# Moving the operands of every large matmul to multiples of 512 bytes

## The chip, the cores and the metric

The kernel runs on one core of a Trainium2 chip. What counts is the device time of one execution in microseconds (us), as the median of several runs. Five engines work side by side from queues of their own: TensorE (PE; its weight loads are shown apart, as PEld), VectorE (DVE), ScalarE (ACT), GpSimd (POOL) and SyncE (SP, which here only issues DMAs). SBUF is the on-chip memory from which all of them read: 128 partitions, each a row of bytes with addresses of its own. In this text the offset of a buffer is the place in that row where it begins.

## The reference

One layer over 256 tokens of width 2048, all in float32: a mixer with three recurrent branches, a cross attention over 256 memory tokens, and a gated feed-forward part. Each is wrapped in an RMS norm and added back.

```python
h = rms_norm(x, norm_mix_pre)
z = h @ w_in                                  # 2048 -> 14368 columns
y_a = gated_delta_rule(...) @ w_dn_out        # chunks of 64 tokens, triangular solves
y_b = gla_chunked(...) @ w_gla_out
y_c = split(gelu(s5_ssm(...)) @ w_s5_glu)
x = x + rms_norm((g_a*y_a + g_b*y_b + g_c*y_c) @ w_mix_out, norm_mix_post)
x = x + rms_norm(cross_attention(rms_norm(x), rms_norm(mem), w_xa_q, w_xa_kv, w_xa_out), norm_xa_post)
gate, up = split(rms_norm(x, norm_ffn_pre) @ w_ffn_up)          # 2048 -> 2 x 5632
x = x + rms_norm((gelu(causal_conv(gate)) * up) @ w_ffn_down, norm_ffn_post)
```

## The kernel before

Nearly all of the arithmetic is matrix products with weights that are read once from HBM. Each float32 factor is split into a high part, rounded to the matmul type float32r, and the rest (`whi`/`wlo` for weights, the two halves of `aa`, `ach`/`acl` and others for activations). A product is then three matmuls: high by high, high by low, low by high.

`load_w` (L198 on) brings two slices of 128 rows by 512 columns into `raw`, and ACT and DVE split them into `whi` and `wlo` (both on L204). Two routines use them:

- `proj` (L226) keeps the weights stationary. `mm3` (L207) issues for each 128x128 block one matmul with `whi`, through which both halves of the activation run as two separate stretches of 256 columns (L216, at the end of a sum L219), and one with `wlo`, through which the high half runs, 256 columns (L217). Such a wide and narrow matmul are called a pair here. There are 64 pairs in a slab of 512 output columns.
- `proj_tok` (L263) keeps the activation stationary and lets 512 columns of `whi`, `whi` and `wlo` run through it, each in one stretch (L283, L284, L285). For a part of `w_kv` it is 256 columns.

The stages follow each other: the columns of `w_in` by `proj` and `proj_tok`, with the recurrent branches in pieces between their matmuls; the branches' output products (with stationary tiles of the pool `s16`, named `f`, and of `aa`); `w_mix` (stationary `mgx`); the cross attention (`aa`, `xq`, `xo_`); 22 slabs of `w_up` by `proj` (moving `aa`); four slabs of `w_down` by `proj_tok` (stationary `ach` and `acl`).

Where a buffer lies is set by the tile pools. A pool of the left side begins where the pool below it ends, one of `side="right"` ends where the one above it begins, and each buffer begins at the next multiple of 32 bytes. The order in which instructions stand on each engine is set when the program is built. In the program as built these are the offsets, as the rest after division by 512:

| buffer | used by | rest before |
|---|---|---|
| `whi`, `wlo` | every product | 96 |
| `aa` | stages up to `w_up` | 96 |
| `f` (`s16`) as stationary | output product of the first branch | 96 |
| `xset`, `xq`, `mgx`, `ach`, `acl` | first stage, attention, `w_mix`, `w_down` | 480 |
| `xo_` | attention output | 64 |

Slices of these buffers begin at further multiples of 512, so all operands taken from one of them share its rest. 96 and 480 are odd multiples of 32; 64 is a multiple of 64.

Of the kernel before, what the change touches and what calls it, by code (L numbers as in the profile page):

```python
# [9 lines left out]
F32 = mybir.dt.float32  # L10
FR = mybir.dt.float32r
# [7 lines left out]
P = 128  # L19
T = 256  # L20
# [3 lines left out]
NW = 512  # L24
# [31 lines left out]
V_CONV = 64  # L56
# [6 lines left out]
V_LIM = V_LRE + 32  # L63
V_LST = V_LIM + 32
V_N = V_LST + 32


def _constants():
# [18 lines left out]
class Net:  # L87
# [21 lines left out]
    def setup(self):  # L109
        self.cp = self.ctx.enter_context(self.pool("cp"))  # L110
        self.ps_acc = self.ctx.enter_context(self.pool("ps_acc", bufs=N_ACC, space=PSUM))
        self.ps_mx = self.ctx.enter_context(self.pool("ps_mx", bufs=8 - N_ACC, space=PSUM))
        self.dram = self.ctx.enter_context(self.pool("dram", space=DRAM))
        self.cst = self.cp.tile([P, C_N], F32, name="cst")
        self.vec = self.cp.tile([P, V_N], F32, name="vec")
        self.ident = self.cst[:, C_ID:C_ID + P]
        self.ones = self.cst[:, C_ONE:C_ONE + P]

# [887 lines left out]
def tile_kernel(ctx, tc, consts, vecs, ab, gla_up, s5_br, s5_bi, s5_cr, s5_ci, post_rows,  # L1006
                x_tok, xT, memT, w_in, w_small, w_dn, w_gla, w_glu, w_mix, w_q, w_kv, w_xo, w_up, w_down, out):
    nc = tc.nc
    n = Net(ctx, tc)
    n.setup()  # L1010
    n.open_weights()
    dram = n.dram
    hpool = ctx.enter_context(n.pool("hp"))

    def set_a(dt=FR):
        return hpool.tile([P, 2, KD, T], dt, name="aa", tag="aa")
# [18 lines left out]
    def xr(k, m=1):  # L1035
        return xh2[k // 8][:, k % 8:k % 8 + m, :] if m > 1 else xh2[k // 8][:, k % 8, :]
# [7 lines left out]
    def x_load(c):  # L1044
        a, b = chs[c]
        nc.sync.dma_start(out=xr(a, b - a), in_=xT[:, a:b, :])

    def hold_dma(ap):
        with n.after(n.prev):
            nc.vector.memset(ap, 0.0)  # L1050

    def x_split():
        for c, (a, b) in enumerate(chs):
            if c < 4:
                x_load(c + 1)
            for k in range(a, b):
                nc.scalar.activation(xs_[:, 0, k, :], xr(k), AF.Copy, scale=n.v_(V_MIXPRE, k))
                n.seq(lambda: nc.vector.scalar_tensor_tensor(xs_[:, 1, k, :], xr(k), n.v_(V_MIXPRE, k),
                                                             xs_[:, 0, k, :].bitcast(F32), op0=ALU.mult,
                                                             op1=ALU.subtract))  # L1060
                made0.append(k)
                yield 0.4
            if c == 3:
                hold_dma(n.cst[:, 0:1])
                nc.sync.dma_start(out=n.cst, in_=consts)
            if c == 4:
                hold_dma(n.vec[:, V_CONV:V_CONV + 1])
                nc.sync.dma_start(out=n.vec[:, V_CONV:], in_=vecs[:, V_CONV:])
            if c:
                a = max(b - 4, 0)  # L1070
                n.norm_acc(n.s4, xr(a, 4).rearrange("p k s -> p (k s)"), xacc, c == 1)
            yield 1.1
# [16 lines left out]
    x_load(0)  # L1089
    nc.sync.dma_start(out=n.vec[:, :V_CONV], in_=vecs[:, :V_CONV])  # L1090
    e0 = n.spawn(x_split(), R_X)
    n.hp = 0
    n.seq_on = True
# [158 lines left out]
    cc = c_stack.enter_context(n.pool("cc"))  # L1252
# [3 lines left out]
    xn = cc.tile([P, 2, D], F32, name="xn")  # L1256
    n.side.dma_start(out=xn, in_=x_tok.rearrange("(t p) e -> p t e", t=2))
    kT = cc.tile([P, 4, T], F32, name="kT")
    n.t2 = c_stack.enter_context(n.pool("ct2", bufs=2))

    def post_row(q, s):
# [58 lines left out]

    nb = n.spawn(norm1(), R_N1)
    n.gate = True
    vt = cc.tile([P, 2, NW], F32, name="vt")

    def v_part(c0, c1):
        n.proj_tok(w_kv[1][:, :, c0:c1], KD, lambda k: (mh[:, k, :], ml[:, k, :]),
                   lambda t, acc: nc.scalar.activation(vt[:, t, c0:c1], acc, AF.Copy, scale=rm_col[:, t:t + 1]),
                   c1 - c0)
# [2 lines left out]
           lambda m, acc: nc.vector.tensor_mul(kT[:, m, :], n.total(acc), rm_row))  # L1331
    if VS:
        v_part(0, VS)
    qT = cc.tile([P, 4, T], F32, name="qT")

    def q_rhs(k):
        n.finish(nb, lambda: k in made)
# [9 lines left out]
    at = cc.tile([P, KD, T], F32, name="at", tag="yg")  # L1347
    pr_ = at[:, 0:8, :].rearrange("p (h t) s -> p h t s", h=4)
    pT = at[:, 8:16, :].rearrange("p (h m) s -> p h m s", h=4)
    xo_ = cc.tile([P, 2, 4, T], FR, name="xo_")  # L1350
    xoh, xol = xo_[:, 0], xo_[:, 1]
    with tc.high_priority(HPA):
        for h in range(4):
# [218 lines left out]
```

## Time and profile before

| | |
|---|---|
| median of three runs | 1955.02 us (1954.22 to 1959.61) |
| the profiled execution's own time | 1953.59 us |
| its span, first to last instruction | 1951.8 us |
| PE busy | 1889.8 us (97%) |
| DVE busy | 1420.0 us (73%) |
| ACT busy | 951.8 us (49%) |
| DMA engines busy, mean | about 60% |
| granted TensorE clock, mean | 0.992 |

The time a matmul is shown to take includes the way through the array and overlaps the next one, so a busy PE tells little of its pace. The pace is read from the starts: the distance from one matmul's start to the next in an unbroken run.

### The profile page before, as it was taken

The page shows a single profiled execution, that of the slowest core. Times are in us where ns is not written, and L with a number is a line of the kernel's source. Part 1 is how long each engine was busy: PE and PEld are TensorE (multiplying, and loading weights), DVE is VectorE, ACT ScalarE, POOL GpSimd, SP SyncE. Part 2 cuts the span into 40 slices and gives each one's busy share as a digit, 9 for nine tenths or more (in the row PEclk, how much of TensorE's full clock was granted, in tenths as well). Part 3 has the DMA queues.
Part 4 walks back from the last instruction along what each step waited for, and adds up shares of the span by engine and source line. Part 5 has one row for each costly group of instructions (what it writes and reads, how often), then busy time and mean ns, then how long its engine had stood idle before and what let it go on. Part 6 is the DMA issues. An engine that isn't in the chain of part 4 may idle for free.

```text
span 1951.8 us, 28177 instructions
## 1 busy us (share of the span) xinstructions
PE 1889.8 (97%) x10440; PEld 1566.7 (80%) x10440; DVE 1420.0 (73%) x2719; ACT 951.8 (49%) x1426; POOL 67.6 (3%) x117
## 2 busy tenths in 40 slices
PE   7989899999999999999999997999999999999997
PEld 6778788777777688878877986888888888888886
DVE  6868999996479999967666756767666676644444
ACT  5655444343564444444455655555545555443432
POOL 0000012020000000000000000000000000000000
PEclk9999999999999999999999998999999999999999
DMA  7535477684445575666576544655665555766664
GB/s 251 176 104 173 150 194 238 187 259 132 125 125 165 182 218 181 214 219 203 185 264 208 174 154 141 218 174 182 197 189 188 184 184 173 237 202 196 192 191 130
DMA packets 107482, 363.93 MB, mean 186 GB/s; under 512 B 12320, under 2 KB 20896, under 8 KB 106832
## 3 DMA queue, kind: packets, MB, share of 16 engines
q1 hardware_dynamic: 97696, 328.32, 54.6%
q0 software_dynamic: 9648, 33.81, 5.5%
q8 instruction: 82, 1.34, 0.3%
q14 instruction: 56, 0.46, 0.1%
HBM read 350.47 MB, written 11.61 MB: 186 GB/s over the span
## 4 chain that ended last, share of the span: by engine, by line
PE 75%; issue 5%; DVE 2%; DMA 2%; POOL 1%; ACT 1%; DVEq 0%; POOLq 0%; ACTq 0%; SPq 0%
PE acc L216 21%; PE acc L285 12%; PE acc L283 12%; PE acc L284 12%; PE acc L217 11%; PE acc L219 1%; PE mx L920 1%; DVE wlo L204 1%; PE mx L181 0%; PE mx L945 0%; PE mx L639 0%; DMA f<-Rd 0%; DMA mch<-in 0%; DMA Xd<-f 0%; PE mx L717 0%
## 5 line engine op out<-in xcount | busy, mean ns | idle before, releaser
L204 DVE TENSOR_TENSOR wlo<-raw,whi 128x1024 fp32r<-128x1024 f32 (+1 forms) x632 | 753.2, 1195 | 426.6 <-ACT whi L204 424.5
L204 ACT CAST whi<-raw 128x1024 fp32r<-128x1024 f32 (+1 forms) x632 | 646.2, 1029 | 738.4 <-PE acc L284 385.3
L216 PE MATMUL acc<-aa,whi 128*128 128x512 f32 x2085 | 725.8, 400 | 12.4 <-DVE r L224 9.6
L217 PE MATMUL acc<-aa,wlo 128*128 128x256 f32 x2224 | 555.5, 284 | 10.7 <-DVE wlo L204 10.7
L217 PEld LDWEIGHTS acc<-aa,wlo 128*128 128x128 f32 x2224 | 422.2, 190 | 54.5 <-DVE wlo L204 22.4
L216 PEld LDWEIGHTS acc<-aa,whi 128*128 128x128 f32 x2085 | 386.0, 190 | 83.1 <-issue 12.3
L283 PE MATMUL acc<-whi,aa 128*128 128x512 f32 (+1 forms) x704 | 269.8, 384 | 0.0
L284 PE MATMUL acc<-whi,aa 128*128 128x512 f32 (+1 forms) x704 | 268.6, 382 | 0.0
L285 PE MATMUL acc<-wlo,aa 128*128 128x512 f32 (+1 forms) x704 | 253.9, 386 | 4.5 <-DVE wlo L204 4.4
L285 PEld LDWEIGHTS acc<-wlo,aa 128*128 128x128 f32 x704 | 131.9, 188 | 36.8 <-DVE wlo L204 10.7
L284 PEld LDWEIGHTS acc<-whi,aa 128*128 128x128 f32 x704 | 132.4, 188 | 26.4 <-issue 1.1
L283 PEld LDWEIGHTS acc<-whi,aa 128*128 128x128 f32 x704 | 132.3, 188 | 26.1 <-issue 1.2
L284 PE MATMUL acc<-whi,acl 128*128 128x512 f32 x352 | 138.9, 395 | 0.0
L283 PE MATMUL acc<-whi,ach 128*128 128x512 f32 x352 | 138.9, 395 | 0.0
L285 PE MATMUL acc<-wlo,ach 128*128 128x512 f32 x352 | 125.4, 395 | 0.0
L930 DVE TENSOR_TENSOR mm<-M,X 128x128 f32<-128x128 f32 x254 | 98.5, 388 | 5.4 <-ACT X L924 0.6
L285 PEld LDWEIGHTS acc<-wlo,ach 128*128 128x128 f32 x352 | 66.3, 188 | 15.5
L283 PEld LDWEIGHTS acc<-whi,ach 128*128 128x128 f32 x352 | 66.3, 188 | 15.5
L284 PEld LDWEIGHTS acc<-whi,acl 128*128 128x128 f32 x352 | 66.3, 188 | 15.4
L932 DVE TENSOR_TENSOR X<-X,s__864 128x64 f32<-128x64 f32 x255 | 71.3, 280 | 4.5
L931 DVE TENSOR_TENSOR s__864<-mm 128x64 f32<-128x64 f32 x255 | 56.4, 221 | 4.7
L224 DVE TENSOR_TENSOR r<-r,acc 128x256 f32<-128x256 f32 x143 | 57.1, 414 | 0.7 <-ACT r L223 0.6
(454 smaller groups left out, 1870.3 us busy)
## 6 DMA issues: line engine op xcount, KB each, us to landing
raw<-in SPq DMA_DIRECT2D x600, 512.0 KB, 4.3
raw<-in SPq DMA_DIRECT2D x32, 256.0 KB, 2.7
gd<-r POOLq DMA_DIRECT2D x24, 256.0 KB, 4.4
f<-gd POOLq DMA_DIRECT2D x12, 512.0 KB, 5.7
f<-Rd POOLq DMA_DIRECT2D x4, 512.0 KB, 6.3
f<-in POOLq DMA_DIRECT2D x4, 512.0 KB, 3.6
gp<-in POOLq DMA_DIRECT2D x8, 256.0 KB, 4.7
xn<-in POOLq DMA_DIRECT2D x1, 2048.0 KB, 11.1
```

The costliest lines, as they stand in the source:

```text
L204: self.last = (nc.scalar.copy(hi, raw), self.seq(lambda: nc.vector.tensor_sub(lo, raw, hi.bitcast(F32))))
L216: nc.tensor.matmul(two, hi, x, start=start, stop=False)
L217: nc.tensor.matmul(two[:, 0, :], lo, x[:, 0, :], start=False, stop=False)
L219: nc.tensor.matmul(two, hi, x, start=start, stop=True)
L224: self.nc.vector.tensor_add(r, r, acc[:, 0:T])
L283: nc.tensor.matmul(accs[t], xh[:, ts_], hi[:, kk, :], start=(kt == 0), stop=False)
L284: nc.tensor.matmul(accs[t], xl[:, ts_], hi[:, kk, :], start=False, stop=False)
L285: last[:] = [nc.tensor.matmul(accs[t], xh[:, ts_], lo[:, kk, :], start=False, stop=(kt == KT - 1))]
L920: nc.tensor.matmul(ps[:, n, c, :], self.Bl[c][rs, ft, :], su[rs, ft, tk], start=True, stop=True, tile_position=(32 * q, 0))
L930: nc.vector.tensor_mul(m, self.M, prev[:, None].broadcast_to([P, 2, 2, 32]))
L931: nc.vector.tensor_add(s, m[:, :, 0, :], m[:, :, 1, :])
L932: nc.vector.tensor_add(X[:, :, :, t], X[:, :, :, t], s)
```

## The change

Two pads and a new order of buffers; no instruction is added, removed or moved. The tile `vec` grows by 104 floats, which lifts all pools of the left side above it by 416 bytes. A tile `edge` of 120 floats, which nothing uses, is put at the end of the right side, and pushes the pools there down by 480 bytes. In the pool `cc` the tiles `vt`, `qT` and `xo_` are made right behind `kT`, ahead of the small ones, so that these no longer shift them. A DMA into `vec` gets an explicit end, so that it moves what it moved.

In the program as built each engine has the same instructions in the same order with the same waits, and all buffers of the table above begin at a multiple of 512. What does not is `cst` (rest 128 before and after), which holds the identity for the transposes, and the diagonal tile of L1370 in the attention (288 after).

```diff
+V_PAD = 104
+R_PAD = 120
...
-        self.vec = self.cp.tile([P, V_N], F32, name="vec")
+        self.vec = self.cp.tile([P, V_N + V_PAD], F32, name="vec")
...
+    n.edge = ctx.enter_context(n.pool("edge", side="right")).tile([P, R_PAD], F32, name="edge")
...
-                nc.sync.dma_start(out=n.vec[:, V_CONV:], in_=vecs[:, V_CONV:])
+                nc.sync.dma_start(out=n.vec[:, V_CONV:V_N], in_=vecs[:, V_CONV:])
...
     kT = cc.tile([P, 4, T], F32, name="kT")
+    vt = cc.tile([P, 2, NW], F32, name="vt")
+    qT = cc.tile([P, 4, T], F32, name="qT")
+    xo_ = cc.tile([P, 2, 4, T], FR, name="xo_")
...
-    vt = cc.tile([P, 2, NW], F32, name="vt")
...
-    qT = cc.tile([P, 4, T], F32, name="qT")
...
-    xo_ = cc.tile([P, 2, 4, T], FR, name="xo_")
```

## Rows read from the trace of the kernel before

**Rows 1.** The page: span, and each engine's busy time, share and instructions.

```profile
span 1951.8 us, 28177 instructions
PE 1889.8 (97%) x10440; PEld 1566.7 (80%) x10440; DVE 1420.0 (73%) x2719; ACT 951.8 (49%) x1426; POOL 67.6 (3%) x117
```

**Rows 2.** The page: chain that ended last, by engine and by line.

```profile
PE 75%; issue 5%; DVE 2%; DMA 2%; POOL 1%; ACT 1%; DVEq 0%; POOLq 0%; ACTq 0%; SPq 0%
PE acc L216 21%; PE acc L285 12%; PE acc L283 12%; PE acc L284 12%; PE acc L217 11%; PE acc L219 1%; PE mx L920 1%; DVE wlo L204 1%; PE mx L181 0%; PE mx L945 0%; PE mx L639 0%; DMA f<-Rd 0%; DMA mch<-in 0%; DMA Xd<-f 0%; PE mx L717 0%
```

**Rows 3.** Matmuls by line, tiles and shape: count, busy us, mean ns, idle before.

```profile
L216 PE MATMUL acc<-aa,whi 128*128 128x512 f32 x2085 | 725.8, 400 | 12.4 <-DVE r L224 9.6 <-DVE s__864 L931 2.2 <-DVE aa L1292 0.4
L217 PE MATMUL acc<-aa,wlo 128*128 128x256 f32 x2224 | 555.5, 284 | 10.7 <-DVE wlo L204 10.7
L283 PE MATMUL acc<-whi,aa 128*128 128x512 f32 x640 | 251.2, 393 | 0.0
L283 PE MATMUL acc<-whi,ach 128*128 128x512 f32 x352 | 138.9, 395 | 0.0
L283 PE MATMUL acc<-whi,mgx 128*128 128x512 f32 x128 | 50.8, 397 | 1.4 <-ACT whi L204 1.4
L283 PE MATMUL acc<-whi,f 128*128 128x512 f32 x64 | 25.0, 391 | 0.0
L283 PE MATMUL acc<-whi,aa 128*128 128x256 f32 x64 | 18.5, 296 | 0.0
L283 PE MATMUL acc<-whi,xo__10518 128*128 128x512 f32 x32 | 12.0, 401 | 0.0
```

**Rows 4.** Stretches: PE, PEld, DVE, ACT, POOL busy (count), granted clock, DMA share, GB/s.

```profile
1300.00:1650.00 350.00, 350.00 (x1979) 301.12 (x1978) 236.62 (x365) 178.89 (x276) 0.00 (x0) 1.00 0.60 187
1700.00:1930.00 230.00, 230.00 (x991) 186.49 (x990) 108.22 (x98) 92.11 (x100) 1.10 (x2) 1.00 0.66 196
350.00:400.00 50.00, 46.26 (x192) 34.89 (x192) 50.00 (x71) 19.05 (x20) 2.42 (x5) 1.00 0.62 187
20.00:240.00 220.00, 203.62 (x1217) 174.31 (x1216) 185.94 (x494) 116.19 (x185) 4.29 (x7) 0.98 0.53 161
650.00:700.00 50.00, 50.00 (x227) 37.33 (x226) 46.59 (x124) 22.83 (x37) 3.85 (x6) 1.00 0.67 204
```

**Rows 5.** PE in order of time (start, us): 512 columns, stationary `f` (rest 96).

```profile
826.20 0.39 PE L285 MATMUL acc<-wlo,f 128*128 128x512 f32 x1
...
829.15 0.39 PE L283 MATMUL acc<-whi,f 128*128 128x512 f32 x1
```

**Rows 6.** The same: 256 columns in one stretch, stationary `aa` (rest 96).

```profile
1135.24 0.28 PE L285 MATMUL acc<-wlo,aa 128*128 128x256 f32 x1
...
1137.04 0.28 PE L285 MATMUL acc<-wlo,aa 128*128 128x256 f32 x1
```

**Rows 7.** The same: 256 columns of `xset` (rest 480), only 32 columns of weights.

```profile
38.70 0.28 PE L1109 MATMUL acc<-xset,f 128*32 128x256 f32 x1
...
40.40 0.28 PE L1109 MATMUL acc<-xset,f 128*32 128x256 f32 x1
```

**Rows 8.** The same, in `w_down`: 512 columns, stationary `ach`/`acl` (rest 480).

```profile
1749.91 0.40 PE L283 MATMUL acc<-whi,ach 128*128 128x512 f32 x1
...
1754.09 0.39 PE L284 MATMUL acc<-whi,acl 128*128 128x512 f32 x1
```

**Rows 9.** The same, in `w_mix`: 512 columns, stationary `mgx` (rest 480).

```profile
999.65 0.40 PE L283 MATMUL acc<-whi,mgx 128*128 128x512 f32 x1
...
1003.38 0.40 PE L283 MATMUL acc<-whi,mgx 128*128 128x512 f32 x1
```

**Rows 10.** The same, attention output: 512 columns, stationary `xo_` (rest 64).

```profile
1159.67 0.39 PE L283 MATMUL acc<-whi,xo__10518 128*128 128x512 f32 x1
...
1162.47 0.39 PE L285 MATMUL acc<-wlo,xo__10518 128*128 128x512 f32 x1
```

## The prediction

> **What bounds the kernel now.** I read the page's engine line first: TensorE is busy for 1889.8 of 1951.8 us, VectorE for 1420.0 [rows 1]. The chain of waits gives PE 75% of the span, and nearly all of that to five lines, the float32r matmuls of `proj` and `proj_tok` [rows 2]. The reader is to see there that the time is the sum of the paces of these matmuls. Then the stretches: from 1300 to 1650 us and from 1700 to 1930 us PE is never idle, at a granted clock of 1.00, so at 2.4 GHz, while DVE works 68% and 47% of the time and the DMA engines 60% and 66% [rows 4]. There the pace of a matmul is the only thing that counts. It isn't so everywhere: in 350 to 400 us DVE is busy for all of the 50 us and PE for 46.26, from 20 to 240 us PE is busy for 203.62 of 220 and DVE for 185.94, and in 650 to 700 us both are nearly full, 50.00 and 46.59 [rows 4].
>
> **The pace, and what is over.** The mean durations (391 to 401 ns for 512 columns) [rows 3] overlap; the distances of the starts are what a matmul costs. Running one column a clock, 512 columns take 213.3 ns and 256 take 106.7 ns. Measured:
> - 256 columns in one stretch, only 32 columns of weights: 15 distances in 1.70 us [rows 7], 113.3 ns, 6.6 over.
> - 256 columns, 128 columns of weights: 15 in 1.80 us [rows 6], 120.0 ns, 13.3 over.
> - 512 columns, stationary at rest 96: 13 in 2.95 us [rows 5], 226.9 ns, 13.6 over.
> - 512 columns, stationary `ach`/`acl` at rest 480: 18 in 4.18 us [rows 8], 232.2 ns, 18.9 over. `mgx`, also 480: 16 in 3.73 us [rows 9], 233.1 ns. `xo_`, rest 64: 12 in 2.80 us [rows 10], 233.3 ns.
> - a pair of `proj`, 768 columns in three stretches and two weight loads: 350 us hold 1979 matmuls [rows 4], so 353.7 ns a pair, 33.7 over 320.
>
> Two things stand out. The excess comes in steps of about 6.67 ns, which at this clock is 16 columns, 64 bytes of float32: one, two, two, nearly three, three, three, and five for the pair. And with the same moving operand (`whi`, rest 96) it depends on where the stationary operand begins: 226.9 against 232 to 233 ns. So the place of an operand does cost time. My reading: the matmul at full rate fetches its columns in pieces of 64 bytes, one per step. A stretch that begins at an odd multiple of 32 (96 and 480 are such) touches one piece more than it has to; a weight load beside it costs a further step, or two when it begins elsewhere in the 512 bytes than the moving operand does.
>
> **The change part by part.** No instruction, order or wait changes, so the whole effect is in these paces. Nothing is added to cost anything: the pads are memory that nobody touches, and the DMA into `vec` has the same bytes. New addresses of what DVE, ACT and the DMAs touch could change their durations too; no row compares two alignments for them, and between 1300 and 1930 us they have a third of their time to spare [rows 4], which would hide either sign there.
>
> With all large operands at multiples of 512, each stretch should save its piece:
> - Pairs: 38 slabs go through `proj` (14 of `w_in`, one of `w_kv`, `w_q`, 22 of `w_up`) at 64 pairs, 2432; 2224 of the narrow ones are the row with `aa` [rows 3]. Three stretches each: 3 x 6.67 = 20 ns, 48.6 us.
> - `proj_tok` with stationary `aa` or `f`, 512 columns: L283 counts 640 and 64, times three lines, 2112 [rows 3]. One piece each: 14.1 us. The 256-column ones, 3 x 64 [rows 3]: 1.3 us.
> - `w_down`, 3 x 352 = 1056 [rows 3]: its stationary operand now begins as the moving one does, so it should reach what `f` has, 226.9, less one piece, 220.2. From 232.2 that is 12.0 ns, 12.7 us. `mgx`, 384: 12.9 ns, 5.0 us. `xo_`, 96: 13.1 ns, 1.3 us.
>
> Sum 83.0 us. The small float32 matmuls of the recurrent branches get nothing: where they are not waiting, I take them as bound by other things.
>
> What of it reaches the end? Until 240 us PE idles for some waits, and 512 of the pairs (10.2 us) lie there; I count half, 5 us lost. From about 280 to 410 us a serial chain on DVE and POOL runs beside 672 matmuls of `proj_tok`, with DVE at 50.00 of 50 us [rows 4]; their 4.5 us are lost whole. From 550 to 800 us DVE is at about 93% [rows 4], so PE can't go much faster before DVE is late; of 256 pairs and 480 matmuls there (8.3 us) I count 4 us lost. That leaves 69.5 us, of which `w_up` alone has 28.2 (1408 pairs) and `w_down` 12.7. In `w_up` DVE would go from 68% to 72%, so nothing new ends last there. From the profiled execution's 1953.59 us this gives 1884.1; the median lies 1.4 us above that execution, so 1885.5 us.
>
> The unknown is how much of the excess goes. The bound above is that all of it goes: 33.7 ns x 2432 + 13.6 x 2112 + 13.3 x 192 + 18.9 x 1056 + 19.8 x 384 + 20 x 96 = 143 us, of which, with the same share lost (69.5 of 83.0), 120 us arrive. The bound below is no gain, or a loss (the last rival). I take one piece a stretch, because the row with the short weight load [rows 7] is the cleanest: one stretch, one piece over, and nothing left to explain.
>
> The Trainium skill's page "TensorE: Matmul & The Clock Gate", section "Back-to-back issue gap", gives N/2.4 + 2.5 ns for warm matmuls, 215.8 for 512 and 109.2 for 256 columns; none of the rows above is that fast. If the change brought all of them there, the sum would be 121 us, of which some 102 would arrive: about 1853 us.
>
> **The rivals.**
> 1. All the excess goes, the step of the weight load too, since both streams then begin at the same place. For it: the excess is a whole number of pieces in most rows [rows 5 to 7], as if nothing else cost anything. Against: 120.0 against 113.3 ns [rows 6, 7] looks like a cost of the load itself, which stays. 1955 - 120 = 1835 us.
> 2. Only the relation of the two operands counts, not 64 bytes. Then `aa`, `f` and the pairs stay (there both begin at 96 now, and both at 0 after), and `ach`, `mgx` and `xo_` fall to 226.9: 1056 x 5.3 + 384 x 6.2 + 96 x 6.4 ns = 8.6 us, 1946.4 us. For it: the one comparison with all else equal [rows 5, 8] is of this kind.
> 3. The step is a fixed cost of each stretch and each load, wherever they begin. Nothing changes: 1955.0 us. For it: no row shows a float32r stream that begins at a multiple of 64, so the piece is inferred. Against: the stationary operand's place matters. The skill's same page (section "Step-by-step: what each phase is for") calls the throughput "purely `N cycles`" and names no address; by that rule this rival holds, and the trace disagrees in so far as 512 columns take 226.9 or 232.2 ns by their place.
> 4. Slower: a load from an aligned place disturbs the stream more. `xo_` is the only stationary operand that begins at a multiple of 64, and its stage is the slowest of all, 233.3 against 226.9 ns [rows 5, 10]. If that is the reason, each matmul with a newly aligned stationary operand pays 6.4 ns: 2112 x 6.4 + 192 x 6.4 + 2432 x 12.8 = 46 us more, up to 2001 us, or 1969 us if the pairs are spared. It decides as soon as the stage with `f` is above 227 ns. Against: `mgx` at rest 480, which isn't a multiple of 64, has 233.1 ns [rows 9].
>
> **How the numbers follow.** The forecast 0.40, with a range of its own of 1862 to 1905 us; all of it 0.20; only the relation 0.13; nothing 0.13; slower 0.14. The predicted time is that of the likeliest, 1885.5 us. The range from 1842 to 1957 us takes in the forecast, most of the first rival, and the second and third; it leaves out the slower case and the far end of the first, under 2 in 10. A measurement of this kernel tells about 0.3%, 6 us, from no change: faster 0.73, same 0.13, slower 0.14.
>
> **What would show it.** After, the stage with `f` at 220 ns and `w_down` at 220 ns (both 227: rival 2; 216 or less: rival 1; 233: rival 4), the narrow matmul of L1109's form at 107 to 109 ns, the pair at about 334 ns in the middle of `w_up`. The stretch of DVE and POOL from 280 to 410 us should take as long as now. I am wrong if the paces don't move, or if they fall and the end doesn't: then DVE or the weight DMAs wait in `w_up`.

## The result and the profile after

The changed kernel took 1944.19 us (median of 4 runs, 1943.77 to 1944.89) against 1956.98 us for the kernel before beside it (4 runs, 1954.22 to 1959.61): ratio 0.9935, 95% interval 0.9918 to 0.9952. Measured twice more on other occasions it came to 0.9945 (0.9932 to 0.9958) and 0.9949 (0.9935 to 0.9962). So it is faster, by half a per cent or a little more. I had forecast 1885.5 us, 3.6% less. The time lies within the wide range, near its upper end, and it is within 0.1% of the second rival's (1946.4 us): that only the place of the two operands relative to each other counts.

The page of the profile after (span; busy time, share and count of each engine; matmul groups) answers to [rows 1, 3]:

```profile
span 1943.1 us, 28177 instructions
PE 1881.5 (97%) x10440; PEld 1567.1 (81%) x10440; DVE 1419.6 (73%) x2719; ACT 952.3 (49%) x1426; POOL 67.4 (3%) x117
...
L218 PE MATMUL acc<-aa,whi 128*128 128x512 f32 x2085 | 727.1, 401 | 11.6 <-DVE r L226 9.6
...
L285 PE MATMUL acc<-whi,ach 128*128 128x512 f32 x352 | 136.9, 389 | 0.0
```

The lines of the code stand two later than before. The pairs' wide matmul (L218) has not become shorter, 401 against 400 ns [rows 3]; only the groups with another stationary operand have, `ach` from 395 to 389 ns. The span fell by 8.7 us and PE is as full as it was.

The stretches of [rows 4] again, in the middle of `w_up` and of `w_down` (PE, PEld, DVE, ACT, POOL busy with counts, granted clock, DMA share, GB/s):

```profile
1300.00:1650.00 350.00, 350.00 (x1978) 301.01 (x1977) 237.98 (x370) 178.73 (x277) 0.00 (x0) 1.00 0.60 186
1700.00:1930.00 230.00, 230.00 (x1016) 190.45 (x1015) 109.28 (x106) 92.19 (x99) 1.10 (x2) 1.00 0.65 192
```

In `w_up` 1978 matmuls start in 350 us, where it was 1979: nothing moved. In `w_down` it is 1016 in 230 us against 991, 2.5% more. Both are at a granted clock of 1.00, as before.

The starts on PE (start, us), for `f` in its own stage, `ach`/`acl`, and `xo_`, as in [rows 5, 8, 10]:

```profile
825.95 0.39 PE L285 MATMUL acc<-whi,f 128*128 128x512 f32 x1
...
827.31 0.39 PE L286 MATMUL acc<-whi,f 128*128 128x512 f32 x1
...
1159.07 0.39 PE L285 MATMUL acc<-whi,xo__9154 128*128 128x512 f32 x1
...
1162.47 0.39 PE L285 MATMUL acc<-whi,xo__9154 128*128 128x512 f32 x1
...
1749.66 0.39 PE L285 MATMUL acc<-whi,ach 128*128 128x512 f32 x1
...
1753.97 0.39 PE L285 MATMUL acc<-whi,ach 128*128 128x512 f32 x1
```

Six distances in 1.36 us, 226.7 ns, with `f` (before 226.9); 15 in 3.40 us, 226.7 ns, with `xo_` (before 233.3); 19 in 4.31 us, 226.8 ns, with `ach` (before 232.2). The three now run alike, and alike means the best pace of before, not a new one.

Where the 8.8 us between the last matmul's start before (1939.3 us) and after (1930.5 us) come from, by the length of the stages in the two traces:

| stage | before, us | after, us | gain |
|---|---|---|---|
| `w_in`, first two runs of `proj` | 234.1 | 234.0 | 0.1 |
| `w_in`, `proj_tok` from 244 us, beside the serial chain | 167.1 | 164.9 | 2.2 |
| all from there to `w_mix` | 567.2 | 566.9 | 0.3 |
| `w_mix` (`mgx`) | 93.5 | 93.3 | 0.2 |
| attention, without its output | 82.2 | 82.2 | 0.0 |
| attention output (`xo_`) | 31.2 | 30.6 | 0.6 |
| `w_up` | 508.8 | 509.4 | -0.6 |
| `w_down` (`ach`) | 245.2 | 239.2 | 6.0 |

These are single profiles. In the three of the changed kernel the time from the end of the serial chain to `w_mix` runs from 565.5 to 568.5 us, so tenths in one row say nothing; and the medians of the three comparisons differ by 12.8, 10.5 and 8.3 us, of which the table accounts for 8.8.

Two things ask for a reason: why alignment gave the pairs nothing, and what became 2.2 us shorter beside the serial chain, where no pace changed (227.7 and 227.5 ns a matmul).

### The profile page after: what moved, and what is told of

The parts are those of the page before. It is cut to its first block, busy times and chain, and to the rows that moved or that the text cites. A ratio compares the mean times of both kernels' runs of the same rounds, so it can differ in the third digit from the quotient of the medians.

```text
span 1943.1 us, 28177 instructions
## 1 busy us (share of the span) xinstructions
PE 1881.5 (97%) x10440; PEld 1567.1 (81%) x10440; DVE 1419.6 (73%) x2719; ACT 952.3 (49%) x1426; POOL 67.4 (3%) x117
## 4 chain that ended last, share of the span: by engine, by line
PE 87%; DVE 7%; issue 4%; DMA 1%; ACT 1%; POOL 0%; SPq 0%; DVEq 0%; ACTq 0%; POOLq 0%
PE acc L218 25%; PE acc L219 14%; PE acc L287 13%; PE acc L285 13%; PE acc L286 13%; DVE wlo L206 2%; PE acc L221 2%; PE mx L922 2%; DVE f L519 1%; DVE mm L932 1%; PE mx L183 0%; PE mx L947 0%; PE mx L641 0%; DVE f L520 0%; DMA mch<-in 0%
## 5 line engine op out<-in xcount | busy, mean ns | idle before, releaser
L218 PE MATMUL acc<-aa,whi 128*128 128x512 f32 x2085 | 727.1, 401 | 11.6 <-DVE r L226 9.6
L218 PEld LDWEIGHTS acc<-aa,whi 128*128 128x128 f32 x2085 | 386.6, 190 | 82.5 <-issue 11.8
L286 PEld LDWEIGHTS acc<-whi,acl 128*128 128x128 f32 x352 | 66.1, 188 | 13.7
L285 PEld LDWEIGHTS acc<-whi,ach 128*128 128x128 f32 x352 | 66.1, 188 | 13.7
L287 PEld LDWEIGHTS acc<-wlo,ach 128*128 128x128 f32 x352 | 66.0, 188 | 13.7
```

The lines of the kernel that those rows point to most:

```text
L218: nc.tensor.matmul(two, hi, x, start=start, stop=False)
L285: nc.tensor.matmul(accs[t], xh[:, ts_], hi[:, kk, :], start=(kt == 0), stop=False)
L286: nc.tensor.matmul(accs[t], xl[:, ts_], hi[:, kk, :], start=False, stop=False)
L287: last[:] = [nc.tensor.matmul(accs[t], xh[:, ts_], lo[:, kk, :], start=False, stop=(kt == KT - 1))]
```

## The experiments

My theory as it stood in the prediction was **A**: a stretch that begins at a multiple of 64 bytes touches one piece less. After the result its rival was **R**: only the distance from the moving to the stationary operand counts (the place of the stationary one less that of the moving one). In every kernel below the instructions, their order and their waits are those of the changed kernel unless it is said.

**All operands at rest 96, none aligned.** If R holds, the gain must come without alignment.

```diff
-V_PAD = 104
-R_PAD = 120
+V_PAD = 0
+R_PAD = 96
```

> The changed kernel with other pads: all large operands (whi, wlo, aa, f, xset, xq, mgx, ach, acl, xo_) begin at rest 96 after division by 512, so at odd multiples of 32, none at a multiple of 64 or 512. Theory R (only the relation of the stationary to the moving operand counts): as the changed kernel, 1944 us, 0.65% faster than before, w_down at 226.7 ns from start to start. Theory A (multiples of 64 or 512 count): as before, 1955 to 1957 us, w_down at about 232 ns.

Measured: 1947.77 us, ratio 0.9963 (0.9952 to 0.9974). PE in `w_down` (start, us):

```profile
1749.40 0.39 PE L285 MATMUL acc<-whi,ach 128*128 128x512 f32 x1
...
1754.16 0.39 PE L285 MATMUL acc<-whi,ach 128*128 128x512 f32 x1
```

21 distances in 4.76 us, 226.7 ns; the stage took 239.2 us as in the changed kernel. At an odd multiple of 32 the whole gain of `w_down` is there.

**Left side at 0, right side at 384: all at multiples of 128, but not alike.**

```diff
-R_PAD = 120
+R_PAD = 24
```

> The changed kernel with a shorter pad on the right: the left side (whi, wlo, aa, f, xo_) at rest 0, the right side (xset, xq, mgx, ach, acl) at rest 384. All are multiples of 128, but the right side stands to the left as it did before the change (480 against 96 is 384). Theory R: w_down back at 232 ns and w_mix at 233 ns, of the gain only that of xo_ stays (0.6 us), 1955 to 1956 us. Theory A: as the changed kernel, 1944 us and 226.7 ns.

Measured: 1951.89 us, ratio 0.9979 (0.9970 to 0.9989). PE in `w_down`:

```profile
1749.62 0.40 PE L285 MATMUL acc<-whi,ach 128*128 128x512 f32 x1
...
1754.04 0.39 PE L285 MATMUL acc<-whi,ach 128*128 128x512 f32 x1
```

19 distances in 4.42 us, 232.6 ns, and 245.2 us for the stage: as before the change. Together the two runs settle it for these matmuls: A falls, R stands. Of the 0.2% that this kernel still gained, 0.6 us are `xo_`, whose operands both lie on the left (30.6 us for the stage, as R had it); the rest belongs to the second question.

**Only one pad, with the distance a multiple of 256.** The left side at 224, the right at 480.

```diff
-V_PAD = 104
-R_PAD = 120
+V_PAD = 32
...
-    n.edge = ctx.enter_context(n.pool("edge", side="right")).tile([P, R_PAD], F32, name="edge")
```

> The smallest pad that makes the rests equal modulo 256: vec grows by 128 bytes, nothing on the right. whi, wlo, aa, f and xo_ begin at rest 224, xset, xq, mgx, ach and acl at 480, all odd multiples of 32. The offsets run showed the same paces at a distance of 0 and of 256 bytes. If the relation modulo 256 is all: w_down at 226.7 ns and 239.2 us, as the changed kernel within 0.1%. If equal rests modulo 512 or multiples of 512 are wanted: w_down stays at 245 us.

Measured: 1947.90 us, ratio 0.9969 (0.9959 to 0.9979), `w_down` 239.2 us. The distance counts modulo 256 bytes; 128 bytes of pad on one side were enough for it.

**The paces by themselves.** A kernel with nothing but matmuls from one buffer of moving and one of stationary columns, 40 in a row for each placement (its output is zeros). The first number is the rest of the moving, the second that of the stationary operand:

```python
for d in range(0, 512, 32):
    one("d" + LET[d // 32], 0, d)
...
for i, r in enumerate((4, 16, 32, 64, 96, 256, 480)):
    one("s" + LET[i], r, r)
...
```

> Only matmuls, none of the kernel's work (the output is zeros): float32r, 40 of a kind in a row, the kinds told apart by the accumulator's name. Moving operand at rest 0, stationary operand of 128 columns at d = 0, 32, ... 480 (da to dp). Theory R: 226.7 ns at d = 0 (and at 512, 1024), 232 to 233 at d = 384 and 480, the others between 220 and 240; both at 4, 16, 32, 64, 96, 256 or 480 (sa to sg): 226.7 all. Theory A: sa to sc, se and sg slower than sd and sf by 6.7 ns. One stretch of 512 against two of 256 (ta to tg): if each stretch costs a step of its own, 226.7 against 233.3. Fewer weight columns at the same rest (la, lb, lc: 32, 64, 96): if the excess comes from the load beside the stream, it falls towards 216 at 32; if it belongs to the stream, it stays at 226.7. Pairs (pa to pp) by d: 351 at d = 0.

PE in order of time (start, us; 40 matmuls a row, so the distance of two rows divided by 40 is the pace). `da` to `di` are distances of 0, 32, ... 256 bytes; `sa` to `sd` have both operands at 4, 16, 32, 64; `le` is 256 columns with 128 columns of weights, `lf` with 64; `tf` is 512 columns in two stretches that lie as the halves of `aa` do:

```profile
26.61 9.24 PE L1069 MATMUL da<-mov,sta 128*128 128x512 f32 x40
35.69 9.49 PE L1069 MATMUL db<-mov,sta 128*128 128x512 f32 x40
45.01 9.50 PE L1069 MATMUL dc<-mov,sta 128*128 128x512 f32 x40
...
82.33 9.33 PE L1069 MATMUL dg<-mov,sta 128*128 128x512 f32 x40
91.50 9.49 PE L1069 MATMUL dh<-mov,sta 128*128 128x512 f32 x40
100.83 9.24 PE L1069 MATMUL di<-mov,sta 128*128 128x512 f32 x40
109.90 9.49 PE L1069 MATMUL dj<-mov,sta 128*128 128x512 f32 x40
...
258.43 9.68 PE L1069 MATMUL sa<-mov,sta 128*128 128x512 f32 x40
267.95 9.40 PE L1069 MATMUL sb<-mov,sta 128*128 128x512 f32 x40
277.19 9.27 PE L1069 MATMUL sc<-mov,sta 128*128 128x512 f32 x40
286.29 9.26 PE L1069 MATMUL sd<-mov,sta 128*128 128x512 f32 x40
...
410.59 4.95 PE L1069 MATMUL le<-mov,sta 128*128 128x256 f32 x40
415.38 4.95 PE L1069 MATMUL ue<-mov,sta 128*128 128x256 f32 x40
420.17 4.71 PE L1069 MATMUL lf<-mov,sta 128*64 128x256 f32 x40
424.71 4.70 PE L1069 MATMUL uf<-mov,sta 128*64 128x256 f32 x40
...
498.27 9.23 PE L1069 MATMUL tf<-mov,sta 128*128 128x512 f32 x40
507.34 9.36 PE L1069 MATMUL tg<-mov,sta 128*128 128x512 f32 x40
516.54 14.29 PE L1069 MATMUL pa<-mov,sta 128*128 128x512 f32 x80
530.67 14.30 PE L1069 MATMUL pb<-mov,sta 128*128 128x512 f32 x80
```

At a distance of 0 it is 9.08 us for 40, 227 ns; at 32 and 64 it is 233 and 233.5; at 192 229; and at 256 again 9.07 us, 226.8 ns. From 256 to 480 the values of 0 to 224 repeat within 0.3 ns. (The accumulators here take turns among eight buffers, which also come round after eight placements; but distances of 544, 1024 and 1408 bytes, in other buffers, gave 233.3, 227.3 and 232.5 ns, as 32, 0 and 128 do.) With equal rests of 32 or 64 it is 9.10 us, 227.5 ns: alignment from 32 bytes up plays no part. Below 32 bytes it does, which R had not expected: both at 4, 238 ns, both at 16, 231. Two stretches (`tf`) cost 226.8 ns, no more than one. And 512 columns in one stretch, both operands at rest 0, are still 13 ns over the 213.3 of one column a clock. So there is no piece that a stretch pays for its start. The excess of two steps that [rows 5, 6] show stays at distance 0, with 256 columns too (`le`, 119.8 ns); fewer columns of weights lower it for 256 columns (`lf`, 113.5 ns) as in [rows 7], but not for 512: with 32 columns of weights (d 0) 231 ns were measured.

**Halves side by side.** If a second stretch cost a step, joining the two halves of `aa`, `xset` and `xq` would save it in each pair.

```diff
+        both = x.rearrange("p c s -> p (c s)")
...
-            nc.tensor.matmul(two, hi, x, start=start, stop=False)
...
+            nc.tensor.matmul(acc, hi, both, start=start, stop=False)
...
-        return hpool.tile([P, 2, KD, T], dt, name="aa", tag="aa")
...
+        return hpool.tile([P, KD, 2, T], dt, name="aa", tag="aa").rearrange("p k c s -> p c k s")
```

> The changed kernel with the two halves of aa, xset and xq side by side, so that the wide matmul of proj runs 512 columns in one stretch instead of two of 256. If each stretch costs a step (6.67 ns): the wide matmul goes from 233 to 227 ns, 2432 of them, 16 us less, of which some 13 arrive: 1931 us. If the two stretches cost nothing of their own and the 233 come from the narrow matmul that follows: 1944 us, no change.

Measured: 1946.26 us, ratio 0.9953 (0.9939 to 0.9967), no gain over the changed kernel. The middle of `w_up`, columns as above:

```profile
1300.00:1650.00 350.00, 350.00 (x1978) 301.01 (x1977) 236.50 (x365) 178.91 (x275) 0.00 (x0) 1.00 0.60 188
```

1978 matmuls in 350 us, to the matmul what the changed kernel has. The stretch costs nothing of its own in the kernel either.

**Can the pairs gain at all?** In the kernel of matmuls a pair took 353.2 ns at distance 0 (`pa` above), and 346.7 at 96 and at 224. The activation of `w_up` moved by 32 bytes in its tile makes the distance 224 there; here on top of the kernel with the one small pad:

```diff
-    def set_a(dt=FR):
-        return hpool.tile([P, 2, KD, T], dt, name="aa", tag="aa")
+    def set_a(dt=FR, shift=0):
+        a = hpool.tile([P, 2 * KD * T + 64], dt, name="aa", tag="aa")[:, shift:shift + 2 * KD * T]
+        return a.rearrange("p (c k s) -> p c k s", c=2, k=KD)
...
-    ff = set_a()
+    ff = set_a(shift=8)
```

> e5, and the activation of w_up (ff) moved by 32 bytes inside its tile, so that the weights begin 224 bytes behind it modulo 256. In the offsets run the pair of a wide and a narrow matmul took 346.65 ns at that distance and 353.1 at 0. If it holds in the kernel: 1408 pairs x 6.45 ns = 9.1 us less in w_up (508.8 to about 500 us), 1935 us in all, 0.45% under the changed kernel. If the real stream, with changing addresses, behaves otherwise: w_up at 509 us and 1944 us.

Measured: 1943.68 us, ratio 0.9944 (0.9932 to 0.9956), beside 0.9969 without the shift. The middle of `w_up`:

```profile
1300.00:1650.00 350.00, 350.00 (x1990) 303.08 (x1989) 241.26 (x378) 180.28 (x282) 0.00 (x0) 1.00 0.60 187
```

1990 matmuls for 1980: 351.8 ns a pair instead of 353.5. `w_up` took 506.8 us instead of 508.7, so 1.9 us, where 6.5 ns x 1408 pairs = 9.1 us were expected. The direction holds, the size doesn't.

**More placements**, 24 in a row of each, to see why: with pairs the distances of wide and narrow matmul were set apart.

> Only matmuls again (the output is zeros), 24 of a kind in a row. Weight columns 64 and 32 under 512 moving columns by distance d (ga to gh, ha to hh): if the two steps over 512 columns belong to the load, some distance gives 33 or 32.5 steps of 6.67 ns (217 to 220 ns); if they belong to the stream, 226.7 is the least. 256 columns by d (ka to kh): 120.0 at d = 0. The pair with the two loads at distances of their own (paa to phh): if 52 steps (346.7 ns) is a floor, none is below; if the two distances act one by one, some cells give 340. Two wide and two narrow ones in a row (va to vh): 696.7 at 0. Loads that change between two distances (wa to wh): 226.7 for equal ones, more for the others.

PE in order of time (24 pairs a row; `paa` and `pab` have the wide one at distance 0, the narrow one at 0 and 32):

```profile
134.59 8.48 PE L1058 MATMUL paa<-mov,sta 128*128 128x512 f32 x48
142.91 8.50 PE L1058 MATMUL pab<-mov,sta 128*128 128x512 f32 x48
```

`paa` is the very pair of `pa` above, yet it took 8.32 us for 24, 346.7 ns, not 353.2. So the same operands at the same places have more than one steady pace, and for pairs their distance does not fix the time. What does is open: the two rows also differ in what ran before them and in the buffer of the accumulator, and neither was tried apart. It may be why a table of paces taken by itself promised 9.1 us and the kernel gave 1.9.

The other rows: the 64 combinations of two distances for a pair ran from 340.0 to about 353 ns, so 346.7 is no floor, but only the one with 64 for the wide and 0 for the narrow matmul came to 340.0, so the two do not act one by one either. With 64 or 32 columns of weights no distance gave less than 227.9 ns; the 217 to 220 of an excess that belongs to the load did not come. And 256 columns took 120.0 ns at distance 0 and 116.7 to 120.0 at the others: there 0 is not the best, so R holds as measured for 512 columns on 128 columns of weights. Loads that alternate between two distances took 227.7 ns when these are equal and 230 to 234.8 when not, as expected.

**The second question.** The kernel with aligned but unlike operands gained 0.2% where R gives it the 0.6 us of `xo_`, and the kernels with the left side at 96 or 224 fell about 0.2% short of the changed one. The stretch of the serial chain goes along with that: 165.1 us in the first, 166.1 and 168.1 in the two others, 164.9 to 165.5 in three profiles of the changed kernel. (It is not all: `w_mix` took 91.5 us in the first, 2 us less than before, at the pace of before, and that stays open.) In this stretch POOL's queue fetches `f<-Rd`, `f<-Ld` and `f<-Xd` into tiles of the pool `s4`, one after the other with work of DVE between. Theory D: these transfers land later when their tiles don't begin at a multiple of 64. To test it, `s4` alone goes back to 96, in the changed kernel:

```diff
         self.t1 = self.main_stack.enter_context(self.pool("t1", bufs=8))
+        self.s4.tile([P, 24], F32, name="shift", tag="shift", bufs=1)
```

> The changed kernel with one unused tile of 96 bytes in the pool s4, so that only the small tiles f of s4 (and what lies above them) begin at rest 96 again, while all operands of the large matmuls stay at rest 0. The paces of matmuls must stay 226.7 ns. Theory D (the small transfers of the delta rule into these tiles land later when they don't begin at a multiple of 64): f<-Ld lands after about 6 us instead of 5.2, the stretch from 244 to 411 us gets 2 to 3 us longer (165 to 167 or 168), and the whole 0.1 to 0.2% slower than the changed kernel, ratio near 0.9963. Rival N (the 3 us in that stretch are not from these tiles): ratio 0.9945 as the changed kernel.

> The changed kernel once more, as the yardstick of this call: ratio 0.9945 to the kernel before, within 0.001.

Measured side by side: 1948.69 us, ratio 0.9967 (0.9954 to 0.9979), against 0.9949 (0.9935 to 0.9962) for the changed kernel; the intervals overlap a little, but the stretch took 167.6 us against 165.5, `w_down` 239.2 in both. DMA queues from 244 to 411 us (packets, MB, share of 16 engines) and issues (count, KB each, median us to landing), first of the changed kernel, then with `s4` at 96:

```profile
q0 software_dynamic: 2281, 6.34, 12.2%
f<-Ld POOLq DMA_DIRECT2D x8, 32.0 KB, 5.8
```

```profile
q0 software_dynamic: 2198, 6.25, 14.0%
f<-Ld POOLq DMA_DIRECT2D x8, 32.0 KB, 6.4
```

Fewer packets of POOL's queue took more of the engines' time. The same views of all profiles:

| kernel | rest of `s4` | stretch, us | share of POOL's queue | `f<-Ld` landing, us |
|---|---|---|---|---|
| before | 96 | 167.1 | 13.6% | 5.9 |
| all at 96 | 96 | 166.1 | 13.7% | 6.3 |
| one small pad | 224 | 168.1 | 14.0% | 6.0 |
| the same, `w_up` shifted | 224 | 167.6 | 14.4% | 6.5 |
| changed, `s4` at 96 | 96 | 167.6 | 14.0% | 6.4 |
| changed, three profiles | 0 | 164.9, 165.1, 165.5 | 11.9%, 12.2%, 12.2% | 5.4, 5.2, 5.8 |
| left 0, right 384 | 0 | 165.1 | 12.5% | 5.3 |
| halves side by side | 0 | 165.2 | 12.7% | 5.3 |
| changed, `w_up` shifted | 256 | 165.1 | 12.8% | 5.3 |

All eleven profiles fall into two groups without a mixture, though some lie close: 165.5 and 166.1 us for the stretch, 5.8 and 5.9 us for the landing. So the run points to the place where the tiles of `s4` begin for the 2 us, with one profile to each layout but the changed one. (The pool `t1` above it moved by the same 96 bytes and was not tried apart; that the transfers into `s4` take longer points to `s4`.)

Where in the stretch they arise, the loop of DVE over the 31 rows of the triangular solve tells (durations in ns; first and last start), again first in the changed kernel, then with `s4` at 96:

```profile
L520 DVE TENSOR_REDUCE f<-f x31: 140/406/1136, 323.8 to 396.9; 64x1 f32<-64x1 f32 x1, 64x2 f32<-64x4 f32 x1, 64x3 f32<-64x9 f32 x1, 64x4 f32<-64x16 f32 x1
L521 DVE TENSOR_REDUCE f<-f x31: 136/401/1136, 326.0 to 399.1; 64x1 f32<-64x1 f32 x1, 64x2 f32<-64x4 f32 x1, 64x3 f32<-64x9 f32 x1, 64x4 f32<-64x16 f32 x1
```

The loop takes 73.1 us in both, and from its last start to the end of the stretch it is 13 us in both, so neither the loop on the moved tiles nor `f<-Xd`, which is issued after it, makes the difference. The 2.2 us lie before the loop: `f<-Rd` is first issued at 279.4 and 279.3 us, `f<-Ld` at 311.6 and 314.2. In these two profiles it is `f<-Rd` and the work up to `f<-Ld` that got longer, more than `f<-Ld` itself.

**The transfers by themselves**, one at a time, each awaited before the next (the output is zeros):

> Transfers only, one at a time, each waited for before the next; the output is zeros. Forms: r* (64 rows by 16 pieces of 256 bytes, 256 KB, as f<-Rd), l* (8 rows by 32 pieces of 128 bytes, 32 KB, as f<-Ld), w* (512 KB of weights, pieces of 2048 bytes); then r and l again as x* and y* beside a running stream of 512 KB weight loads. The last letter is the rest at which the row in SBUF begins: a 0, b 32, c 64, d 96, e 128, h 224. Theory D: b, d and h (not multiples of 64) land 0.5 us or more later than a, c and e in the forms r and l, little in w. Rival N: all six the same within 0.1 us, and the differences between the kernels come from what else is under way.

Issues of the form of `f<-Ld` (the last number is the median landing, us; `la`, `lc`, `le` at rest 0, 64, 128, `lb`, `ld`, `lh` at 32, 96, 224):

```profile
la<-in POOLq DMA_DIRECT2D x8, 32.0 KB, 2.6
lb<-in POOLq DMA_DIRECT2D x8, 32.0 KB, 2.8
lc<-in POOLq DMA_DIRECT2D x8, 32.0 KB, 2.7
ld<-in POOLq DMA_DIRECT2D x8, 32.0 KB, 2.8
le<-in POOLq DMA_DIRECT2D x8, 32.0 KB, 2.5
lh<-in POOLq DMA_DIRECT2D x8, 32.0 KB, 2.8
```

Multiples of 64 land in 2.5 to 2.7 us, the others in 2.8. The direction is D's, the size is 0.1 to 0.3 us, not the 0.5 and more that I expected. The same form beside the stream of weight loads, from 919 to 1629 us (the last three of the eight repeats ran after the stream had ended, and there the times are those above within 0.1 us):

```profile
ya<-in POOLq DMA_DIRECT2D x5, 32.0 KB, 5.0
yb<-in POOLq DMA_DIRECT2D x5, 32.0 KB, 6.0
yc<-in POOLq DMA_DIRECT2D x5, 32.0 KB, 5.0
yd<-in POOLq DMA_DIRECT2D x5, 32.0 KB, 5.4
ye<-in POOLq DMA_DIRECT2D x5, 32.0 KB, 4.9
yh<-in POOLq DMA_DIRECT2D x5, 32.0 KB, 5.4
```

Here the multiples of 64 land in 4.9 to 5.0 us and the others in 5.4 to 6.0, 0.4 us or more later, which is about D's size; these are medians of five, and single transfers overlap. The 256 KB form shows nothing of the kind: alone 14.1 to 14.2 us at five rests and 18.5 at rest 0, which came right behind the 512 KB loads; beside the stream 17.1, 16.9, 17.1 us at 0, 64, 128 and 16.9, 16.7, 16.6 at 32, 96, 224. The 512 KB form can't be read, since its loads ran into one another. So D is borne out for the form of `f<-Ld` beside other traffic; why the part of the chain with `f<-Rd` gets longer in the kernel is not shown. The Trainium skill's page "DMA: Bandwidth & Descriptors", section "How a descriptor splits into AXI transactions", has transfers split at multiples of 256 bytes, and a start off these cost extra beats on the reading side. Applied to the written side, rests 32, 64, 96 and 224, at each of which every second piece of 128 bytes crosses such a multiple, would be alike and worse than 0 and 128; the rows beside the stream have 64 with 0 and 128 instead.

**Both put together:** the changed kernel with `w_up`'s activation shifted by 32 bytes (the diff of the shift as above).

> The changed kernel with the activation of w_up shifted by 32 bytes in its tile (distance 224 there). If what e4_up_32_bytes gave over e5_one_small_pad (w_up 506.8 against 508.7 us) adds to the changed kernel: about 1.9 us less than it, ratio near 0.9935, time near 1942. If the pace that a run of pairs settles into depends on more than this distance, w_up may stay at 508.6 and the ratio at 0.9945.

Measured: 1942.64 us, ratio 0.9935 (0.9922 to 0.9947), beside 0.9949 for the changed kernel on the same occasion; `w_up` 506.7 us against 508.6 to 509.4 in its three profiles:

```profile
1300.00:1650.00 350.00, 350.00 (x1990) 303.07 (x1989) 240.78 (x378) 180.73 (x283) 0.00 (x0) 1.00 0.59 186
```

The two effects add. Its median is the lowest of all these kernels, though the intervals overlap with the changed one's; the stage times show the 2 us, the medians alone would not.

The changed kernel had been run again beside the one small pad, too:

> The changed kernel once more, beside the next two on one chip. The stages that moved (w_down 245.2 to 239.2 us, the attention output 31.2 to 30.6) give 0.34%; the first comparison gave 0.65%, interval 0.48 to 0.82. If only the relation of the operands counts: 0.3 to 0.5% faster than before. If addresses at multiples of 512 also help something else (the weight DMAs, the serial stretch from 244 to 411 us): 0.6% again, and more than the next kernel by 0.2%.

It gave 1943.98 us, 0.9945, beside 0.9969 for the small pad, whose `w_down` is just as short. In the profiles of these two 3.0 us of the difference are the stretch of the serial chain, as in the table above.

## Why the prediction was wrong, point by point

- **What bounds the kernel** was right: PE's pace decides, and a pace that fell came through whole where PE never waits (`w_down`, 6.0 us; 5.6 by the second rival's sum).
- **The step that failed** is the sentence "a stretch that begins at an odd multiple of 32 touches one piece more than it has to". The steps of 16 columns in the paces are there, but I gave them a cause that the rows could not show, and the row that I took for the cleanest [rows 7] differs from [rows 6] in the weight columns and from the rest in the number of columns too. With both operands at rest 0, where there is no piece to save, 256 columns keep the same excess: 119.8 ns with 128 columns of weights and 113.5 with 64. In the kernel the whole run of L1109's form went from 115.0 to 115.9 ns, not to 107 to 109. The terms that hung on it, 48.6 us of pairs, 14.1 of `proj_tok` and 1.3 of its short form, 64 of 83 us, measured nothing: 1978 matmuls for 1979 in `w_up`, 226.7 for 226.9 ns with `f`. The run with all at rest 96 and the one with halves side by side show it from both sides. In its place the runs showed that the distance of the two operands modulo 256 bytes sets the pace of 512 columns: 232.4 to 226.7 ns for `ach`, at rest 96 as at 0, and back at 232.6 with both aligned but unlike.
- **Half of the w_down term** was right. I had 12.7 us, 5.6 for the relation and 7.1 for the piece; the relation came.
- **`mgx`**: the relation's 2.4 us did come in the pace (232.8 to 227.3 ns), but the stage kept 93.3 of 93.5 us. The group after:

```profile
L285 PE MATMUL acc<-whi,mgx 128*128 128x512 f32 x128 | 50.1, 391 | 3.2 <-ACT whi L206 3.2
```

  PE now waits 3.2 us for ACT's `whi` where it waited 1.4 [rows 3]: the 1.8 us went into that wait. In the prediction I had asked what is late next for `w_up` only; here it was ACT, which in this stretch also waits for the transfer `mch` (8.6 us after, 7.4 before).
- **The second rival** had the mechanism and the one comparison with all else equal. I gave it 0.13, although I named what spoke for it. Its 8.6 us sum became 6.8 of its own (`w_down` 6.0, `xo_` 0.6, `mgx` 0.2) and 2.2 us that no rival had, from the serial chain.
- **That DMA durations could move with the addresses** I did write, and covered it only for 1300 to 1930 us, where nothing waits for them. In the serial chain, where I expected no change from 280 to 410 us, the chain waits for them, and that stretch became 2.2 us shorter.
- **The rule of the Trainium skill** that I weighed (page "TensorE: Matmul & The Clock Gate", section "Back-to-back issue gap", 215.8 ns for 512 columns; the section calls this the gap of an isolated matmul and has about 131 ns for a stream of weight loads and matmuls): no placement measured here came near either; the best is 226.7 ns, also in the kernel of matmuls, where no other engine works beside PE. The account in the page's section "Step-by-step: what each phase is for", that throughput is purely a matter of columns, names no address; the 226.7 to 238 ns here for the same columns do not agree with it.
- **Left open**: what the remaining excess is, two steps of 16 columns for a matmul of 512 columns at the best placement and 33 ns a pair, what puts a row of pairs into the one or the other steady pace, and how the place of the `s4` tiles lengthens the chain. For the excess, neither the number of stretches nor alignment nor the weight columns alone account for it.

## What to carry to other kernels

A pace that comes in even steps doesn't tell what a step is: before a sum is built on a reading, it needs two rows that differ in that one thing alone, and where the trace has just one such pair of rows, the forecast should go by what that pair shows. For float32r matmuls of 512 columns on 128 columns of weights, keep both operands at multiples of 32 bytes and the stationary one a multiple of 256 bytes from the moving one; alignment beyond that gave these matmuls nothing. Where small transfers stand in a serial chain, let their tiles begin at multiples of 64 (the kernel was tried with 0 and 256 against 96 and 224, the transfers by themselves with 64 and 128 too), and judge a layout change stage by stage, since the paces and the chain answer to different buffers.

## What was unexpected in the hardware

- The pace of a float32r matmul of 512 columns depends on the distance between its two operands modulo 256 bytes: 226.8 ns at 0, 229 at 192, 232.5 to 233.8 at the others, 128 among them. With 256 columns 0 is not the best: 120.0 ns, and 116.7 at 224.
- Below 32 bytes the place itself counts: both operands at 4 bytes, 238 ns; at 16, 231 ns; from 32 on, at equal places, 227.
- The same pair at the same places ran steadily at 346.7 ns in one kernel and at 353.2 in another; what decides is open.
- With the tiles of `s4` at 96 or 224 instead of 0 or 256, POOL's transfers had 13.6 to 14.4% of the DMA engines' time in the stretch from 244 to 411 us instead of 11.9 to 12.8%, and the stretch was about 2 us longer.
- A transfer of 32 KB in pieces of 128 bytes, beside a stream of weight loads, landed in 4.9 to 5.0 us at rests 0, 64 and 128 and in 5.4 to 6.0 at 32, 96 and 224; alone it is 2.5 to 2.7 against 2.8.
